# Moving the group-end output stores of a decoder-layer kernel from ScalarE to SyncE, and spreading them over the next group

## Chip, cores and metric

The kernel runs on all 8 cores of one Trainium2 chip; each core does an eighth of the tokens and shares nothing with the others. The metric is the device time of the slowest core, in microseconds (us).

An 8-core program has two states on this chip. In the fast state all cores grant TensorE a clock of about 0.98 to 0.99 of full speed on average. In the slow state the cores of one die (0 to 3 or 4 to 7) are granted less, and the whole takes some per cent longer.

## The reference

One layer over two kinds of request. Cut to what matters here:

```python
def layer(x):                                  # prompt rows, then decode rows
    n = rmsnorm(x) * norm1_g
    q, k, v, u, gates = project(n, w_in)       # u = GLU, 1024 channels
    ya = sliding_window_attention(q, k, v)     # decode rows also read cache_k, cache_v
    yc = silu(layernorm(depthwise_conv31(u)))  # decode rows also read state_conv
    h = x + (gates[0] * (ya @ w_attn_o) + gates[1] * (yc @ w_conv_o)) @ w_out
    h = h + square(relu(rmsnorm(h) @ w_up)) @ w_down
    return rmsnorm(h) * norm_f_g               # y, the output of this study
```

## The kernel before

A core works through its tokens in three groups (640, 768 and 704 columns, the last with 64 decode tokens). All activations lie transposed in SBUF: `H` is 16 chunks of 128 rows, one column a token. Weights stream through five slots in 110 slabs a group; GpSimd issues them. Each engine takes its instructions in program order, as the timelines below show. A helper adds the semaphore waits (an engine waits for a counter that another engine or a landing transfer raises) from what an operation reads and writes. For buffers in SBUF it compares byte ranges; for a tensor in DRAM it knows only the name:

```python
def keys(self, ap):
    name = ap.tensor.name
    if name not in self.base:                  # not in SBUF
        return [name]                          # one key for the whole tensor
    ...                                        # else: its 128-byte pieces
```

The 16 stores of a group write different parts of one tensor, `y`. To the helper they all write the same thing, so each store gets a wait for the landing of the store before it.

The end of a group scales `H` in place by the last norm and stores it as `y`. These tasks are put on a list, `side`, and are taken one at a time between the next group's first matmul groups (K, V, Q):

```python
def final_tasks(g):
    def fin(): ...                             # 1 / rms of H into LR
    def out(k):
        if k < 16:
            stt(H[:, k, 0:M], H[:, k, 0:M], v1(V_GF + k), LR[:, 0:M], ALU.mult, ALU.mult)   # VectorE
        if k > 0:
            P.dma("act", yo[g][:, k - 1, :], H[:, k - 1, 0:M], f"d_y{k - 1}")               # ScalarE
    return [fin] + [lambda k=k: out(k) for k in range(17)]
```

So every `step()` in K, V, Q puts one store on ScalarE's queue, between two evictions of PSUM banks:

```python
for j in range(8):                             # Q; K and V have the same form
    ...
    for c0, n in CH:
        b = fm(w, j % 2, nT, halo + c0, n)     # 16 matmuls into one of 8 PSUM banks
        act(qo[:, j, c0:c0 + n], b[:, 0:n], AF.Copy)   # ScalarE empties the bank
        step()
```

What follows K, V, Q reuses the bytes of `H`, which is why a chunk's store has a deadline:

```python
gt  = over(H, 0 ...)              # chunks 0, 1       GLU
cw  = over(H, 4096 ...)           # chunk 1           conv weights, one buffer
um  = over(H, 6144 ...)           # chunks 2 to 4     GLU outputs, three buffers
KcT = over(H, 5 * HB ...)         # chunks 5 to 7     cached keys      (last group only)
vcb = over(H, 5 * HB + 8192 ...)  # chunks 7 to 10    cached values    (last group only)
stb = over(H, 5 * HB + 16384 ...) # chunks 10 to 12   cached conv state (last group only)
tA, tB = ...                      # chunks 8 to 11, 12 to 15   gates, after GLU
```

Each of eight GLUs computes 128 channels. SyncE then makes 16 small copies (the shift), each 32 partitions, that lay the channels out for the convolution on TensorE; conv(m-1) runs behind GLU m, so a shift has one GLU's time:

```python
def sample_load():                             # last group, before GLU in this kernel
    P.dma("pool", KcT, ckT); P.dma("pool", vcb, cvT)

def glu(m):
    wl = slab() ...                            # GpSimd: load of a later slab
    ...
    for i in range(4):
        for q in range(4):
            P.dma("sp", z[32*i:32*i+32, q, 0:L-3], u[32*q:32*q+32, i:i+L-3], ...)   # shift

def conv(m):
    P.dma("pool", cw, cwd[m], "d_cw")          # GpSimd
    ...                                        # 64 or 96 matmuls

for m in range(8):
    glu(m)
    if m >= 1:
        conv(m - 1)
```

The softmax here doesn't subtract the row's maximum and nothing guards it: scores larger than these inputs give would overflow.

Of the kernel before, what the change touches and what calls it, by code (L numbers as in the profile page):

```python
# [9 lines left out]
ALU = mybir.AluOpType  # L10
# [10 lines left out]
GROUPS = [(0, 5, 128, 0), (5, 6, 0, 0), (11, 5, 0, NSMP)]  # L21
WMAX = 768
SEQW = 36
M_OUT = list(range(8)) + [10, 11, 14, 15, 8, 9, 12, 13]
ULEN = 32 + 640 + 16 * SEQW
NSLOT = 5
V_G1, V_G2, V_GF, V_BG, V_CB, V_LG, V_LB, V_SK, V_N = 0, 16, 32, 48, 80, 88, 96, 104, 120
# [134 lines left out]
def chunks_of(n):  # L162
    k = -(-n // 512)
    step = -(-n // (k * 32)) * 32
    return [(c, min(step, n - c)) for c in range(0, n, step)]


def build():
    nc = bass.Bass("TRN2", target_bir_lowering=False)
    es = ExitStack()  # L170
    with es:
# [3 lines left out]
        def dout(name, shape):  # L175
            return nc.dram_tensor(name, list(shape), F32, kind="ExternalOutput").ap()
# [15 lines left out]
        yo = [dout(f"y{i}", [128, 16 * m]).rearrange("p (k c) -> p k c", k=16) for i, (w, m) in enumerate(gw)]  # L192
# [7 lines left out]
        P = Prog(nc, es)  # L200
# [4 lines left out]
        def sb(name, shape, dt):  # L205
            t = P.sb(name, shape, dt, at[0])
            n = int(np.prod(shape[1:])) * (4 if dt == F32 else 2)
            at[0] += -(-n // G) * G
            return t
# [5 lines left out]
        H = sb("H", [128, 16, WMAX], F32)  # L215
# [8 lines left out]
        LR = sb("LR", [128, WMAX], F32)  # L224
# [59 lines left out]
        def slab(nk=16):  # L284
            k = nxt[0]
            nxt[0] += 1
            if k > 0:
                load_slab()
            t = wsl[k % NSLOT]
            return t[:, :].rearrange("p (k c) -> p k c", k=nk)  # L290
# [6 lines left out]
        def fm(w, m, act, c0, n, nk=16):  # L297

            b = bank()
            mm(b[:, 0:n], [(w[:, k, m * 128:(m + 1) * 128], act[:, k, c0:c0 + n]) for k in range(nk)])  # L300
            return b

        def act(out, in_, func, **kw):
            P.op("act", "activation", out=out, in_=in_, func=func, **kw)

        def stt(out, in0, scalar, in1, op0, op1):
            P.op("dve", "scalar_tensor_tensor", out=out, in0=in0, scalar=scalar, in1=in1, op0=op0, op1=op1)
# [4 lines left out]
        def v1(c):  # L312
            return vec[:, c:c + 1]
# [4 lines left out]
        def step(n=1):  # L318
            for _ in range(n):
                if side:  # L320
                    side.pop(0)()

        def drain():
            while side:
                side.pop(0)()
# [15 lines left out]
        def rstd(r, s, c0, n):  # L341

            b = bank()
            mm(b[:, 0:n], [(onesf[:, :], s[:, c0:c0 + n])])
            act(r[:, c0:c0 + n], b[:, 0:n], AF.Sqrt, bias=EPS)
            P.op("dve", "reciprocal", out=r[:, c0:c0 + n], in_=r[:, c0:c0 + n])

        def add_square(dst, src, first, c0, n, t=None):
            t = sq[:, c0:c0 + n] if t is None else t
            if first:  # L350
                act(dst[:, c0:c0 + n], src, AF.Square)
            else:
                act(t, src, AF.Square)
                tt(dst[:, c0:c0 + n], dst[:, c0:c0 + n], t, ALU.add)
# [11 lines left out]
        for hf in range(2):  # L366
# [3 lines left out]
            for k in range(16):  # L370
                c = slice(hf * half, hf * half + half)
                stt(nT[:, k, c], H[:, k, c], v1(V_G1 + k), R1[:, c], ALU.mult, ALU.mult)

        def norm1_tasks(g):

            W = gw[g][0]

            def p1(k):
                P.dma("sp", xr[k % 3][:, 0:W], xin[g][:, k, :], f"d_xr{k % 3}")
                add_square(R1, xr[k % 3][:, 0:W], k == 0, 0, W)  # L380

            def fin():
                for c0, n in chunks_of(W):
                    rstd(R1, R1, c0, n)

            def p2(k):
                P.dma("sp", xr[(k + 1) % 3][:, 0:W], xin[g][:, k, :], f"d_xr{(k + 1) % 3}")
                stt(nT[:, k, 0:W], xr[(k + 1) % 3][:, 0:W], v1(V_G1 + k), R1[:, 0:W], ALU.mult, ALU.mult)

            return ([lambda k=k: p1(k) for k in range(16)] + [fin] + [lambda k=k: p2(k) for k in range(16)])  # L390

        def final_tasks(g):
            M = gw[g][1]

            def fin():
                for c0, n in chunks_of(M):
                    rstd(LR, S2, c0, n)

            def out(k):
                if k < 16:  # L400
                    stt(H[:, k, 0:M], H[:, k, 0:M], v1(V_GF + k), LR[:, 0:M], ALU.mult, ALU.mult)
                if k > 0:
                    P.dma("act", yo[g][:, k - 1, :], H[:, k - 1, 0:M], f"d_y{k - 1}")

            return [fin] + [lambda k=k: out(k) for k in range(17)]

        for g, (b0, nb, halo, ns) in enumerate(GROUPS):
            first, last = g == 0, g == len(GROUPS) - 1
            W, M = gw[g]
# [104 lines left out]
            def sample_load():  # L514
                P.dma("pool", KcT[:, :, :, :], ckT[:, :].rearrange("p (a b w) -> p a b w", a=2, b=16), "d_kc")
                P.dma("pool", vcb[:, :, :], cvT[:, :].rearrange("p (b c) -> p b c", b=16), "d_vc")
# [39 lines left out]

            side += [lambda i=i, a=a: unit(i, a) for i in range(nb) for a in range(2)] + [flush]
            if last:
                sample_load()
                side += [sample_q] + [lambda a=a, hh=hh: sample_unit(a, hh) for a in range(2) for hh in range(2)]  # L560


# [2 lines left out]
            UC = chunks_of(W - us)  # L565
            L = 32 + Mp + (16 * SEQW if last else 0)
            if last:
                P.dma("pool", stb[:, :, :, :], stT[:, :].rearrange("p (k b r) -> p k b r", k=8, b=16), "d_st")

            def seqs(ap):  # L570
                return ap.rearrange("p (b r) -> p b r", r=SEQW)

            def glu(m):
                u = um[m % 3]
                wl = slab()
                if not first:
                    P.op("act", "copy", out=u[:, 0:32], in_=cuT[:, m, :])
                if last:
                    P.op("pool", "tensor_scalar", out=seqs(u[:, 32 + Mp:L])[:, :, 0:32], in0=stb[:, m, :, :],
                         scalar1=2.0, scalar2=None, op0=ALU.mult)  # L580
                for ci, (c0, n) in enumerate(UC):
                    bB = fm(wl, 0, nT, us + c0, n)
                    step(ci == 0)
                    bA = fm(wl, 1, nT, us + c0, n)
                    t = gt[ci % 2]
                    act(t[:, 0:n], bB[:, 0:n], AF.Tanh, scale=0.5)
                    pe = min(c0 + n, Mp) if last else c0 + n
                    if pe > c0:
                        stt(u[:, uoff + c0:uoff + pe], t[:, 0:pe - c0], 1.0, bA[:, 0:pe - c0], ALU.add, ALU.mult)
                    if last:  # L590
                        sv = max(c0, Mp)
                        if sv < c0 + n:
                            s0, s1 = sv - Mp, c0 + n - Mp
                            assert s0 == 0 and s1 == 64
                            stt(seqs(u[:, 32 + Mp:L])[:, :, 32:36],
                                t[:, sv - c0:n].rearrange("p (b t) -> p b t", t=4), 1.0,
                                bA[:, sv - c0:n].rearrange("p (b t) -> p b t", t=4), ALU.add, ALU.mult)
                        o0 = max(c0, Mp - 30)
                        if o0 < c0 + n:
                            stt(ucs[:, m, o0 - Mp + 30:c0 + n - Mp + 30], t[:, o0 - c0:n], 1.0, bA[:, o0 - c0:n],  # L600
                                ALU.add, ALU.mult)
                    step(ci == 1)
                if not last:
                    P.op("act", "copy", out=cuT[:, m, :], in_=u[:, Mp:Mp + 32])
                z = ush[m % 2]
                for i in range(4):
                    for q in range(4):
                        P.dma("sp", z[32 * i:32 * i + 32, q, 0:L - 3], u[32 * q:32 * q + 32, i:i + L - 3],
                              f"d_ul{m % 2}{i}{q}", merge=(i + q > 0))
# [24 lines left out]

            for m in range(8):
                glu(m)
                if m >= 1:
                    conv(m - 1)
            drain()
# [72 lines left out]

            for i, m in enumerate(M_OUT):
                if i % 2 == 0:
# [14 lines left out]
            if not last:  # L729
                side += norm1_tasks(g + 1)  # L730
            ri = 0
            for fb in range(4):
# [13 lines left out]
                for m in range(16):  # L746
# [8 lines left out]
                    if m % 2 == 1:  # L755
                        step(1)
            drain()
            side += final_tasks(g)
        drain()
        P.emit()  # L760
    return nc


def _cols(w, cols):
    k = w.shape[0] // 128
    return w[:, cols].reshape(k, 128, len(cols)).transpose(1, 0, 2).reshape(128, 4096)


def _slabs(w_in, w_ao, w_co, w_out, w_up, w_dn):
# [16 lines left out]
    for j in range(0, 16, 2):  # L786
        s.append(_cols(w_out, r(256) + M_OUT[j] * 128))
    for fb in range(4):
# [109 lines left out]
```

## Time and profile before

| | before |
|---|---|
| runs at the time of the prediction | 3565.6, 3725.5, 3942.8 us (only the first is fast) |
| profiled run, fast | 3558.2 us; cores 3539.9 to 3556.6 us |
| TensorE busy | 3376.2 us of 3556.6 |
| first border (K, V, Q of group 1), median of cores | 78.0 us |
| second border (K, V, Q of group 2) | 97.0 us |
| GLU and conv of group 1, of group 2 | 157.3 us, 162.0 us |
| the 16 last stores, after TensorE has ended | 36.2 us |

The four stage times are worked out from the timelines of the profiled run, core by core, then the median of the eight is taken. A border runs from the first matmul that sums the previous group's last norm (it sits behind K's first 16 matmuls) to ScalarE's first copy of the carried conv state; the GLU stretch goes on from there to the first matmul of the layer-norm sums.

TensorE is the bound, so what can be won is its idle time. These are the waits of TensorE in the kernel before, core 2, first in the window 1090 to 1210 us and then in 2330 to 2460 us. The columns are: engine, what it was to write, whom it waited for, us in total, number of waits, the longest.

```profile
PE ps L154 <- ACT qo L154: 7.8, 2, 6.2
PE ps L154 <- ACT vtok L154: 7.0, 1, 7.0
...
PE ps L154 <- ACT qo L154: 23.5, 4, 9.1
PE ps L154 <- ACT vst L154: 6.3, 1, 6.3
PE ps L154 <- ACT vtok L154: 1.0, 1, 1.0
```

The releaser of every wait shown is a ScalarE eviction. Why ScalarE was late is in its own timeline (start, duration, engine, operation, in brackets the idle time before and its releaser), here in the second border:

```profile
2407.89 0.34 ACTq L154 DMA_DIRECT2D y<-H  x1
2408.33 0.46 ACT L154 ACTIVATE qo<-ps 128x352 bf16<-128x352 f32 x1 [1.89 <-DMA y<-H]
2421.09 0.34 ACTq L154 DMA_DIRECT2D y<-H  x1
2421.59 0.46 ACT L154 ACTIVATE qo<-ps 128x352 bf16<-128x352 f32 x1 [12.79 <-DMA y<-H]
2434.17 0.34 ACTq L154 DMA_DIRECT2D y<-H  x1
```

A store (ACTq) stands between two evictions. Its own record takes 0.34 us, but the store issued at 2407.89 lets the next one out only at 2421.09, and the eviction behind that one stands in the queue for 12.79 us. The trace has the first landing at 2421.03. On every core of this profile, in 44 or 45 of the 45 pairs of neighbouring stores of one group, the next was issued 0.07 us after the one before had landed, and never before it. TensorE fills the eight banks and stops:

```profile
2393.34 2.55 PE L154 MATMUL ps<-nT,wsl_53 128*128 128x352 bf16 x16 [0.38 <-ACT qo L154]
2401.37 4.61 PE L154 MATMUL ps<-nT,wsl_53 128*128 128x352 bf16 x16 [5.48 <-ACT qo L154]
...
2422.20 4.44 PE L154 MATMUL ps<-nT,wsl_49 128*128 128x352 bf16 x16 [9.05 <-ACT qo L154]
```

The second line shows the other cost of a gap: 16 matmuls take 4.61 us instead of 2.55, because the clock was lowered while TensorE stood (the trace has a granted clock of one half from 2398.8 to 2405.6 us).

The timeline of GpSimd in the last group has the issue of conv 4's weights, `cw`, behind GLU 5's slab:

```profile
2523.30 0.58 POOL L154 DMA_DIRECT2D cw<-cwd  x1
```

And ScalarE's timeline ends with the last 16 stores, after TensorE's last matmul:

```profile
3517.86 36.20 ACTq L154 DMA_DIRECT2D y<-H  x16
```

### The profile page before, as it was taken

To read this page: it belongs to the slowest core of one execution; us is meant where nothing else is said; L and a number is where in the kernel's file an instruction comes from. 1 tells how busy PE (TensorE), PEld (TensorE's weight loads), DVE (VectorE), ACT (ScalarE), POOL (GpSimd) and SP (SyncE) were. 2 spreads that over 40 slices of the span, in tenths; PEclk is the share of its full clock that TensorE was granted. 3 is DMA by queue.
4 is the path that set the end of the run, shared out by engine and by line. 5 is a ranking of instruction groups with operands and counts; after the bars stand their busy time and mean duration, and the time that the engine had idled before them with its cause. 6 is when DMAs were issued, how large, how long until landed. Compare 5 with 4: busy or idle time off the path is not lost.

```text
span 3556.6 us, 61094 instructions; the slowest of 8 cores (3539.9 to 3556.6 us)
## 1 busy us (share of the span) xinstructions
PE 3376.2 (95%) x23732; PEld 2172.0 (61%) x23732; DVE 1162.6 (33%) x1846; ACT 705.5 (20%) x1381; POOL 202.3 (6%) x371
## 2 busy tenths in 40 slices
PE   2999999999999999999999999987999999999994
PEld 1656777777776455666666666654566666666663
DVE  4244133332223354224233222333542242222224
ACT  2322133111021333113211011112231131101021
POOL 0000000000000000000000000001100000000000
PEclk9999999999999999999999999998999999999997
DMA  6779877887666666556666655567776666566661
GB/s 135 118 133 174 161 149 152 161 167 136 119 122 134 125 130 143 106 115 118 137 131 132 122 99 104 101 138 156 142 153 114 126 110 113 107 112 114 108 114 71
DMA packets 98474, 453.52 MB, mean 128 GB/s; under 512 B 14960, under 2 KB 27696, under 8 KB 55472
## 3 DMA queue, kind: packets, MB, share of 16 engines
q0 software_dynamic: 51696, 355.75, 56.5%
q1 hardware_dynamic: 39584, 76.56, 8.0%
q10 hardware_dynamic: 6912, 17.30, 1.3%
q8 instruction: 195, 3.19, 0.4%
q14 instruction: 87, 0.71, 0.1%
HBM read 765.00 MB, written 23.85 MB: 222 GB/s over the span
## 4 chain that ended last, share of the span: by engine, by line
PE 89%; DMA 6%; SPq 2%; DVE 1%; issue 1%; ACT 0%; DVEq 0%; ACTq 0%
PE ps L154 89%; DMA y<-H 4%; SPq L154 2%; DMA H<-x 1%; DMA ush_83<-um_93 0%; DVE H L154 0%; DVE rden_67 L154 0%; DMA ush_82<-um_93 0%; DVE nT L154 0%; DVE LR L154 0%; DVE R_58 L154 0%; DMA ush_83<-um_94 0%; DVE um_93 L154 0%; DVE qo L154 0%; SPq L151 0%
## 5 line engine op out<-in xcount | busy, mean ns | idle before, releaser
L154 DVE TENSOR_TENSOR H<-ps,H 128x320 f32<-128x320 f32 (+2 forms) x384 | 201.5, 525 | 566.4 <-PE ps L154 566.2
L154 PE MATMUL ps<-nT,wsl_49 128*128 128x384 bf16 (+2 forms) x1344 | 217.9, 322 | 19.4 <-ACT qo L154 16.9
L154 PE MATMUL ps<-a2T,wsl_50 128*128 128x320 bf16 (+2 forms) x1344 | 203.9, 313 | 0.0
L154 PE MATMUL ps<-hb,wsl_53 128*128 128x320 bf16 (+2 forms) x1344 | 203.9, 313 | 0.0
L154 PE MATMUL ps<-a2T,wsl_51 128*128 128x320 bf16 (+2 forms) x1344 | 203.9, 313 | 0.0
L154 PE MATMUL ps<-hb,wsl_52 128*128 128x320 bf16 (+2 forms) x1344 | 203.9, 313 | 0.0
L154 PEld LDWEIGHTS ps<-nT,wsl_49 128*128 128x128 bf16 x1344 | 133.3, 100 | 101.8 <-issue 33.9
L154 ACT ACTIVATE a2T<-rt_105 128x320 bf16<-128x320 f32 (+2 forms) x96 | 47.6, 496 | 736.1 <-DVE rt_105 L154 736.1
L154 PE MATMUL ps<-nT,wsl_50 128*128 128x352 bf16 (+2 forms) x1152 | 178.9, 316 | 8.6 <-ACT qo L154 8.6
L154 PE MATMUL ps<-nT,wsl_51 128*128 128x352 bf16 (+2 forms) x1152 | 178.2, 315 | 0.5 <-issue 0.5
L154 DVE SCALAR_TENSOR_TENSOR tA<-tA,ps 128x320 f32<-128x320 f32 (+2 forms) x96 | 50.0, 520 | 387.2 <-PE ps L154 386.7
L154 PE MATMUL ps<-hb,wsl_50 128*128 128x320 bf16 (+2 forms) x1152 | 175.3, 313 | 0.0
L154 PE MATMUL ps<-a2T,wsl_49 128*128 128x320 bf16 (+2 forms) x1152 | 174.8, 313 | 0.0
L154 PE MATMUL ps<-a2T,wsl_52 128*128 128x320 bf16 (+2 forms) x1152 | 174.8, 313 | 0.0
L154 PE MATMUL ps<-hb,wsl_51 128*128 128x320 bf16 (+2 forms) x1152 | 174.8, 313 | 0.0
L154 PE MATMUL ps<-a2T,wsl_53 128*128 128x320 bf16 (+2 forms) x1152 | 174.8, 313 | 0.0
L154 PE MATMUL ps<-hb,wsl_49 128*128 128x320 bf16 (+2 forms) x1152 | 174.8, 313 | 0.0
L154 PEld LDWEIGHTS ps<-hb,wsl_52 128*128 128x128 bf16 x1344 | 131.5, 98 | 69.4 <-issue 0.4
L154 PEld LDWEIGHTS ps<-a2T,wsl_50 128*128 128x128 bf16 x1344 | 131.5, 98 | 69.0
L154 PEld LDWEIGHTS ps<-hb,wsl_53 128*128 128x128 bf16 x1344 | 131.5, 98 | 69.0
L154 PEld LDWEIGHTS ps<-a2T,wsl_51 128*128 128x128 bf16 x1344 | 131.5, 98 | 69.0
L154 PE MATMUL ps<-nT,wsl_52 128*128 128x352 bf16 (+2 forms) x960 | 152.5, 320 | 14.3 <-ACT vtok L154 8.0
(222 smaller groups left out, 4284.0 us busy)
## 6 DMA issues: line engine op xcount, KB each, us to landing
wsl_49<-wst POOLq DMA_DIRECT2D x66, 1024.0 KB, 9.5
wsl_50<-wst POOLq DMA_DIRECT2D x66, 1024.0 KB, 9.5
wsl_51<-wst POOLq DMA_DIRECT2D x66, 1024.0 KB, 9.4
wsl_52<-wst POOLq DMA_DIRECT2D x66, 1024.0 KB, 9.8
wsl_53<-wst POOLq DMA_DIRECT2D x66, 1024.0 KB, 9.5
H<-x SPq DMA_DIRECT2D x8, 768.0 KB, 21.6
cw<-cwd POOLq DMA_DIRECT2D x24, 256.0 KB, 8.6
H<-x SPq DMA_DIRECT2D x16, 384.0 KB, 7.2
```

The lines of the kernel that those rows point to most:

```text
L154: i = getattr(eng, ins[0])(**ins[1])
```

## The change

The intent is to take the stores off ScalarE, which TensorE depends on, and to put them on SyncE, which has next to nothing to do in K, V, Q. Eight stores go there, in the order in which the next group needs the bytes: chunks 0 to 4 for GLU, 10 to 12 for the conv state. The other eight go out one behind each shift. Because `KcT` and `vcb` lie over chunks 5 to 10, of which 5 to 9 are now stored during GLU, their loads move behind GLU 5.

```diff
+Y_OUT = [0, 1, 2, 3, 4, 10, 11, 12, 5, 6, 7, 8, 9, 13, 14, 15]
...
+        stores = []
+        def store():
+            if stores:
+                stores.pop(0)()
...
-            def out(k):
-                if k < 16:
-                    stt(H[:, k, 0:M], ...)
-                if k > 0:
-                    P.dma("act", yo[g][:, k - 1, :], H[:, k - 1, 0:M], f"d_y{k - 1}")
-            return [fin] + [lambda k=k: out(k) for k in range(17)]
+            def out(i, k):
+                stt(H[:, k, 0:M], ...)
+                stores.append(lambda: P.dma("sp", yo[g][:, k, :], H[:, k, 0:M], f"d_y{k}"))
+                if i < 8:
+                    store()
+            return [fin] + [lambda i=i, k=k: out(i, k) for i, k in enumerate(Y_OUT)]
...
             if last:
-                sample_load()
                 side += [sample_q] + ...
...
             for m in range(8):
                 glu(m)
+                store()
+                if last and m == 5:
+                    sample_load()
                 if m >= 1:
                     conv(m - 1)
...
         drain()
+        while stores:
+            store()
```

More of the change, by code (lines that the diff above doesn't have):

```diff
@@ L397, in fin @@
                     rstd(LR, S2, c0, n)
-            def out(k):
-                if k < 16:
-                    stt(H[:, k, 0:M], H[:, k, 0:M], v1(V_GF + k), LR[:, 0:M], ALU.mult, ALU.mult)
-                if k > 0:
-                    P.dma("act", yo[g][:, k - 1, :], H[:, k - 1, 0:M], f"d_y{k - 1}")
-            return [fin] + [lambda k=k: out(k) for k in range(17)]
+            def out(i, k):
+                stt(H[:, k, 0:M], H[:, k, 0:M], v1(V_GF + k), LR[:, 0:M], ALU.mult, ALU.mult)
+                stores.append(lambda: P.dma("sp", yo[g][:, k, :], H[:, k, 0:M], f"d_y{k}"))
+                if i < 8:
+                    store()
+            return [fin] + [lambda i=i, k=k: out(i, k) for i, k in enumerate(Y_OUT)]
         for g, (b0, nb, halo, ns) in enumerate(GROUPS):
```

## The prediction

> Times are for the fast state: of the runs before (3565.6, 3725.5, 3942.8 us) only the first is fast, as is the profiled one (3558). I predict against about 3560, not the median.
>
> **What bounds it.** The summary shows TensorE 95% busy (3376 of 3557 us). It idles about 65 us at the start, 42 after its last matmul, 46 at the two group borders, 17 waiting for conv shifts. The chain of waits puts 4.2% (149 us) on y stores, but TensorE works through most of that; only its idle counts.
>
> In the TensorE waits at the borders (K, V, Q of the next group) the releaser is a ScalarE eviction (vtok, vst, qo): 15 us at the first, 31 us at the second. The ScalarE timeline shows a y store between evictions, and the next instruction often comes only when a store has landed (2.2 us undisturbed, 8 to 13 beside weight loads).
>
> After each gap over 5 us matmuls run slowly: 16 of 352 columns take 4.6 instead of 2.55 us. The Trainium skill (TensorE: Matmul & The Clock Gate, HAM section) says that an idle window of about 3.4 us halves the clock; this trace agrees (granted clock 0.90 and 0.85 in the two stretches). That costs 4.7 and 7.9 us. To be won: 19 + 39 = 58 us on the slowest core, some 50 on others.
>
> **What the change does.** The stores leave ScalarE; else TensorE, ScalarE and VectorE keep their order. SyncE is nearly idle in K, V, Q, so eight stores there are free. Bytes stay the same. It adds:
> 1. SyncE in GLU: a shift (16 copies) occupies it 10.6 to 12.7 us; shifts start every 16 to 19 us, but the last every 13.2 us, when attention has run out. A store of 2.3 to 8 us fits the long gaps, not the last two or three, where TensorE already waits (1 to 3 us each). Estimate: +6 us in group 1, +5 in group 2, at conv 5 to 7.
> 2. Last group: the loads of KcT and vcb move behind GLU 5 on GpSimd's queue, ahead of conv 4's weights (cw). vcb must wait for the store of chunk 9, behind shift 4 (which ended at 2530 us). cw, issued at 2523 us before, is issued near 2535 and lands behind 1 MB loads: from before's landings (16.8, 23.2, 29.2 us, some 7 us apart) I estimate 2546, while conv 4 is due at 2533. A stall of 12 us (10 more than before) plus 3 of low clock: +13 us.
> 3. End: 16 stores on ScalarE took 36 us; on SyncE I expect the same.
>
> **Sum.** 58 - 11 - 13 = 34 us on the slowest core, a little less on others: 3528 us (0.9% faster), 8 in 10 between 3500 and 3556. Faster by over 2%: 3%; within 2%: 95%; slower by over 2%: 2%.
>
> **To check.** TensorE waits on vtok, vst, qo near zero at both borders, clock there about 1.0; K, V, Q with GLU's first matmuls in about 65 and 61 us (before 84 and 97). Waits on ush grow by 2 to 8 us each at the late convs. In the last group one TensorE wait of 8 to 20 us at conv 4, released by cw. Final stores 36 us.
>
> **What would make it wrong.** Stores in GLU much slower than 5 us would push every shift back (up to 30 us lost, no gain). cw may overtake the cache loads, or vcb be issued early (45 to 50 us gained). Final stores could be slower on SyncE. If the slow state falls on most runs, times are hundreds of us higher for other reasons.

## The result

| | before | after |
|---|---|---|
| runs, all | 3559.5, 3565.6, 3725.5, 3942.8 us | 3526.4, 3529.8, 3530.4, 3531.4 us |
| median of all | 3645.6 us | 3530.1 us |
| ratio of fast runs | 1 | 0.9907 (95% interval 0.9883 to 0.9931) |
| cores in the profiled run | 3539.9 to 3556.6 us | 3509.9 to 3528.9 us |
| first border | 78.0 us | 61.6 us |
| GLU stretch of group 1 | 157.3 us | 158.0 us |
| second border | 97.0 us | 58.0 us |
| GLU stretch of group 2 | 162.0 us | 187.0 us |
| last 16 stores | 36.2 us | 35.4 us |

The ratio is the mean time of one kernel's fast runs over that of the other's of the same rounds, so it is not quite the ratio of the medians quoted. The medians of all runs differ by 3%, but two of the four runs before were slow and none of the four after; the change is worth 0.9%.

The stages account for it: 16.4 + 39.0 = 55.4 us won at the borders, 0.7 lost in the first GLU stretch and 25.0 in the second, 29.7 us in all; the medians of the cores' spans in the two profiled runs, about 3548 and 3521 us, differ by 27.

In the profile after, TensorE of core 6 (the slowest) waits for nothing between 1095 and 1175 us, nor between 2300 and 2400 us: the lists of waits are empty. The first border is an unbroken row of matmuls at full clock; three lines of it, from the timeline of TensorE, without any idle time in brackets:

```profile
1131.04 10.56 PE L155 MATMUL ps<-nT,wsl_51 128*128 128x384 bf16 x64
1141.44 10.56 PE L155 MATMUL ps<-nT,wsl_52 128*128 128x384 bf16 x64
1151.84 10.56 PE L155 MATMUL ps<-nT,wsl_53 128*128 128x384 bf16 x64
```

A new wait stands first among the rest of TensorE's waits in the whole run (the start of the kernel left out):

```profile
PE ps L155 <- DMA cw<-cwd: 22.1, 1, 22.1
PE ps L155 <- DMA ush_83<-um_93: 10.4, 3, 6.8
...
PE ps L155 <- DVE ucs L155: 3.2, 1, 3.2
```

All eight cores have it, with 18.8 to 22.8 us. TensorE's timeline shows that it is conv 4, and what follows at low clock (5.04 us; conv 3, with data at hand, took 2.72):

```profile
2470.16 2.72 PE L155 MATMUL ps<-ush_83,cw 128*32 128x320 bf16 x96
...
2505.79 5.04 PE L155 MATMUL ps<-ush_82,cw 128*32 128x320 bf16 x96 [22.11 <-DMA cw<-cwd]
```

GpSimd's timeline shows what `cw` waited for:

```profile
2471.00 0.58 POOL L155 DMA_DIRECT2D KcT<-ckT  x1
2493.09 0.53 POOL L155 DMA_DIRECT2D vcb<-cvT  x1 [21.52 <-issue]
2493.65 0.53 POOL L155 DMA_DIRECT2D cw<-cwd  x1
```

GpSimd stood 21.5 us before it issued `vcb`. It calls the wait "issue", that is, it names no releaser; the chain of waits in the window 2465 to 2512 us names it: the store of chunk 9, which SyncE had issued behind shift 4 and whose bytes `vcb` reuses, and then `cw` behind the cache loads. (Columns: start, us, what.)

```profile
2481.21 8.87 DMA y<-H
2490.11 2.96 issue
...
2493.65 11.47 DMA cw<-cwd
```

SyncE's timeline in GLU of group 1 shows why the stores there cost so little, and its last line the final 16 stores:

```profile
1118.26 44.62 SPq L155 DMA_DIRECT2D y<-H  x8
...
1293.48 11.97 SPq L155 DMA_DIRECT2D ush_82<-um_92  x16
1305.54 0.54 SPq L155 DMA_DIRECT2D y<-H  x1
1306.71 11.51 SPq L155 DMA_DIRECT2D ush_83<-um_93  x16
...
3488.61 35.36 SPq L155 DMA_DIRECT2D y<-H  x16
```

Eight stores in a row hold SyncE for 44.62 us, 5.6 us each. But a single store between two shifts holds it for 0.54 us, and the next shift starts 0.6 us after it. The difference is the helper's wait again. Seven of the eight stores in a row wait for the one before, at line 152 of the kernel, the helper's `wait_ge`; of the final sixteen, fifteen do (SyncE's own waits, core 6, first in the window 1100 to 1190 us, then in 3480 to 3530):

```profile
SPq L152 <- DMA y<-H: 40.7, 7, 9.6
...
SPq L152 <- DMA y<-H: 27.5, 15, 2.0
```

A store in GLU finds that the one before has long landed. The queue itself is not what holds: the 16 copies of a shift, which the helper does not chain, went out 0.75 us apart (from 1293.48 us), while each landed 3.3 to 9.5 us after its issue.

### The profile page after: what moved, and what is told of

It is laid out like the page before. It is cut to its first block, busy times and chain, and to the rows that moved or that the text cites. A ratio compares the mean times of both kernels' runs of the same rounds, so it can differ in the third digit from the quotient of the medians.

```text
span 3528.9 us, 61086 instructions; the slowest of 8 cores (3509.9 to 3528.9 us)
## 1 busy us (share of the span) xinstructions
PE 3366.7 (95%) x23732; PEld 2169.5 (61%) x23732; DVE 1162.5 (33%) x1846; ACT 706.5 (20%) x1381; POOL 202.5 (6%) x371
## 4 chain that ended last, share of the span: by engine, by line
PE 90%; DMA 4%; SPq 2%; DVE 2%; issue 1%; ACT 0%; DVEq 0%; POOL 0%; ACTq 0%; POOLq 0%
PE ps L155 90%; DMA y<-H 2%; SPq L155 2%; DMA H<-x 1%; DVE rden_67 L155 0%; DVE H L155 0%; DMA ush_83<-um_93 0%; DMA cw<-cwd 0%; DMA stb<-stT 0%; DMA ush_83<-um_94 0%; DVE nT L155 0%; DVE LR L155 0%; DMA ush_82<-um_92 0%; DVE R_58 L155 0%; DVE rden_68 L155 0%
## 5 line engine op out<-in xcount | busy, mean ns | idle before, releaser
L155 PEld LDWEIGHTS ps<-nT,wsl_49 128*128 128x128 bf16 x1344 | 132.0, 99 | 81.4 <-issue 13.3
L155 PE MATMUL ps<-nT,wsl_51 128*128 128x352 bf16 (+2 forms) x1152 | 178.2, 315 | 0.0
L155 PE MATMUL ps<-nT,wsl_50 128*128 128x352 bf16 (+2 forms) x1152 | 176.7, 313 | 0.0
L155 PEld LDWEIGHTS ps<-nT,wsl_51 128*128 128x128 bf16 x1152 | 112.5, 98 | 63.3 <-issue 3.7
```

Source lines behind the costliest of these rows:

```text
L155: i = getattr(eng, ins[0])(**ins[1])
```

## The experiments

Theory A says that the borders were long because stores on ScalarE held up evictions; its rival B says that too much was stored in that stretch, whichever engine issued it. Theory C says that the loss in the last group is `cw` standing behind `vcb`, which waits for a store, plus crowding of the DMA engines by the cache loads; its rival D says crowding alone. Three chips served three batches of runs. On the first, even runs counted as fast had dips of clock on a die, the kernel before lying between 3559 and 3599 us; there the stage times of the profiled run say more than the total. The stage times, in us, medians of the cores of one profiled run each:

| kernel | border 1 | GLU 1 | border 2 | GLU 2 |
|---|---|---|---|---|
| before | 78.0 | 157.3 | 97.0 | 162.0 |
| changed | 61.6 | 158.0 | 58.0 | 187.0 |
| changed, run again | 62.1 | 157.6 | 58.0 | 187.2 |
| stores on ScalarE, spread | 69.7 | 158.2 | 72.1 | 177.2 |
| before, stores on SyncE | 61.6 | 175.5 | 58.0 | 198.5 |
| cw first | 61.6 | 157.4 | 58.0 | 172.4 |
| chunk 9 early | 61.6 | 158.1 | 58.0 | 181.2 |
| loads apart, early | 62.2 | 158.6 | 58.4 | 176.3 |
| the same, two queues at the end | 62.0 | 157.7 | 58.3 | 176.8 |
| loads apart, late | 61.6 | 157.8 | 58.0 | 168.5 |
| no cache loads | 61.6 | 158.9 | 58.0 | 175.5 |

### Stores at the new places, but on ScalarE

```diff
-                stores.append(lambda: P.dma("sp", yo[g][:, k, :], ...))
+                stores.append(lambda: P.dma("act", yo[g][:, k, :], ...))
```

> The changed kernel with its stores, at the same places, issued from ScalarE again. Theory A (what counts at the borders is that a store on ScalarE holds up the evictions behind it): eight of sixteen stores still sit between evictions, so some of the border waits come back, TensorE waits on vtok, vst, qo of about 7 us in each border plus low clock, about 19 us for both against 58 before; the wait on cw stays near 20 us; 3540 to 3555 us. Rival B (the gain is that half the stores left the border, whatever engine issues them): no border waits to speak of, 3525 to 3535 us, like the changed kernel.

Measured: ratio to the kernel before 0.9893 (0.9837 to 0.9949); its quiet runs took 3540.3, 3542.0 and 3542.5 us. The waits in the second border, core 7:

```profile
PE ps L155 <- ACT vst L155: 6.1, 1, 6.1
PE ps L155 <- ACT vtok L155: 4.6, 1, 4.6
```

Part of the border loss came back: 8.1 us and 14.1 us over the changed kernel, 22.2 us together against the 19 expected. With half the stores gone from the border but the engine unchanged, about 40% of the loss remains. This speaks for A and against B. In GLU the same stores on ScalarE cost nothing that the table shows (158.2 us in group 1): there the store before has landed.

One expectation failed: the wait on `cw` was not near 20 us but 13.4 to 17.3 us on the eight cores, and the second GLU stretch took 177.2 us, 9.8 less than in the changed kernel. On ScalarE the store of chunk 9 did not stand behind the copies of shift 4: it went out 1.5 us before `KcT`, and in the changed kernel some 10 us after it. This agrees with theory C.

### The kernel before, only the engine changed

```diff
-                    P.dma("act", yo[g][:, k - 1, :], H[:, k - 1, 0:M], f"d_y{k - 1}")
+                    P.dma("sp", yo[g][:, k - 1, :], H[:, k - 1, 0:M], f"d_y{k - 1}")
```

> The kernel before with one word changed: all sixteen stores stay in K, V, Q but are issued from SyncE; cache loads stay where they were. Theory A: the border waits on vtok, vst, qo vanish (58 us won on the slowest core), but the stores occupy SyncE for about 16 x 5.5 = 88 us, longer than the 64 us of K, V, Q, so the first conv shifts start late: about 10 us lost in group 1; in the last group KcT, vcb and stb load late too, about 25 us lost at the first conv. 3520 to 3555 us, with waits on ush at conv 0. Rival B: the same bytes in the same stretch, so no gain, 3555 us or more, with TensorE still waiting in K, V, Q.

Measured: ratio 0.9964 (0.9911 to 1.0017), its quickest run 3556.7 us. The borders are those of the changed kernel to the tenth (61.6 and 58.0 us), with all sixteen stores still issued in a row. That settles A against B: it is enough that the stores, with their waits for each other, leave ScalarE. Not tested is the other remedy, to let the helper tell the chunks of `y` apart and to leave the stores on ScalarE. But SyncE now issues stores until long after the border, and the shifts queue behind them (first the timeline of SyncE, core 7, group 1, then TensorE's waits in that GLU stretch):

```profile
1117.27 99.45 SPq L154 DMA_DIRECT2D y<-H  x16
1216.91 33.03 SPq L154 DMA_DIRECT2D ush<-um  x35
```

```profile
PE ps L154 <- DMA ush<-um: 26.2, 3, 23.7
```

Sixteen stores took 99.45 us and the first shift began at 1216.91. GLU lost 18.2 us in group 1 and 36.5 us in group 2 (in the latter also because the cache loads came late), which is 54.7 of the 55.4 won. So the second half of the change, the spreading, is what keeps the gain. The expectation had 10 and 25 us; the stores in a row, each issued when the one before had landed, were slower (6.2 us each) than the 5.5 assumed.

### Conv weights ahead of the cache loads

```diff
                 store()
-                if last and m == 5:
-                    sample_load()
                 if m >= 1:
                     conv(m - 1)
+                if last and m == 5:
+                    sample_load()
```

> The changed kernel with the loads of KcT and vcb one place later on GpSimd's queue, behind conv 4's cw. Theory C (cw is late because it stands behind vcb, which waits for the store of chunk 9): the wait of 22 us on cw is gone, but vcb itself still waits for that store until about 2490 us and lands about 10 us later, while the first sample unit needs it near 2491: a new wait of about 10 us on vcb. Net 8 to 14 us faster than the changed kernel: 3514 to 3522 us. Rival D (the DMA engines are simply overfull in this stretch): cw stays late by over 10 us, no gain.

Measured: ratio 0.9865 (0.9809 to 0.9920) in a noisy batch, with 3519.5 us in the only run in which both dies were undisturbed. The wait on `cw` is gone (core 4, window 2400 to 2600 us):

```profile
PE ps L155 <- DMA ush<-um: 7.7, 2, 5.1
PE ps L155 <- DMA vcb<-cvT: 1.2, 1, 1.2
```

The GLU stretch fell from 187.0 to 172.4 us, with 174.1 on the die that was undisturbed in the profiled run. So the place of `cw` in GpSimd's queue was about half of the loss of 25.0 us (see the repeat below), against D. A miss of size: the wait on `vcb` was at most 4.1 us on any core, not 10; about 5 us moved to the shift of conv 4, which now shares the DMA engines with the cache loads.

Run again in the third batch:

> The run with cw ahead of the cache loads once more, so that the next two can be compared with it on one chip. It should repeat: last group's GLU stretch (from the first copy of carried conv state to the layer-norm sums) 172 us against 187 in the changed kernel and 162 before; on an undisturbed die about 10 us shorter than the changed kernel's 3521.

Its three fast runs took 3518.5, 3519.2 and 3521.0 us, ratio 0.9876 (0.9856 to 0.9895). The profiled execution was slow, so it is not in the table. But its die 0 (cores 0 to 3) was undisturbed, with a clock of 0.988: the GLU stretch of group 2 took 175.6 us there, not the 172 expected. With both profiles the order of the loads is worth 11 to 15 of the 25 us.

### Chunk 9 stored early

```diff
-Y_OUT = [0, 1, 2, 3, 4, 10, 11, 12, 5, 6, 7, 8, 9, 13, 14, 15]
+Y_OUT = [0, 1, 2, 3, 4, 10, 11, 12, 9, 5, 6, 7, 8, 13, 14, 15]
-                if i < 8:
+                if i < 9:
```

> The changed kernel with chunk 9 stored ninth, still in K, V, Q, so that vcb needs no store behind shift 4; the loads stay ahead of cw. Theory C: vcb is issued right after KcT (about 2471 us), cw about 2472 us; cw still queues behind the slab and both cache loads and lands near 2494: the wait on cw falls from 22 to about 10 us. 8 to 14 us faster than the changed kernel: 3514 to 3522 us. If the whole stall was the wait for the store, it falls below 3 us (3505 us); if it was all queueing, it stays near 20 us.

Measured: ratio 0.9836 (0.9783 to 0.9890), verdict unclear. Four runs without a disturbed die took 3526.7 to 3528.3 us, only 2 to 3 us below the changed kernel's 3530 on another chip, where 8 to 14 were expected; the GLU stretch is 5.8 us shorter. GpSimd no longer waits for the store: `vcb` follows `KcT` after 2.2 us. Yet conv 4 still waits 14.6 us (13.4 to 15.7 on the eight cores), now with the shift named (core 4; TensorE's waits, then GpSimd's timeline):

```profile
PE ps L155 <- DMA ush<-um: 16.8, 3, 14.6
```

```profile
2472.28 0.58 POOL L155 DMA_DIRECT2D KcT<-ckT  x1
2474.48 0.53 POOL L155 DMA_DIRECT2D vcb<-cvT  x1 [1.63 <-issue]
2475.04 0.53 POOL L155 DMA_DIRECT2D cw<-cwd  x1
```

A shift copy issued at 2481.20 us took 19.1 us to land, and `cw` needed 19.3 us, beside a slab and both cache loads, where the medians of the same operations are 8.7 and 9.1 us over the whole stretch (2400 to 2560 us). So crowding is real, too: with the store out of the way, it alone makes a wait of this length. The store wait and the queueing overlap, and the 22 us cannot be split into two parts that add up. The Trainium skill (DMA: Bandwidth & Descriptors, section Queues, rings and completion order) says that a DMA engine goes round the queues that have work, packet by packet, so small copies on another queue share it with large loads; these landings agree, but no run here looks at packets.

### Both remedies: the loads earlier, together or apart

These ran in a second batch, beside the changed kernel once more:

> The changed kernel itself, unedited, once more, to stand beside the next three on the same chip. Both theories: one wait on cw of 19 to 23 us on every core, no wait on vtok, vst or qo; 3526 to 3535 us in fast runs if the chip is as steady as the first one.

Its five fast runs took 3536.0 to 3548.9 us (ratio 0.9913, 0.9873 to 0.9952), and the wait on `cw` was 23.0 us on core 2. The first ratio repeats.

First both loads behind conv 3's `cw`, with chunk 9 early:

```diff
                 if m >= 1:
                     conv(m - 1)
+                if last and m == 4:
+                    sample_load()
```

> Chunk 9 stored ninth, and both cache loads together one GLU earlier, behind conv 3's cw. Theory C (store wait plus crowding): the wait for the store is gone, but 2 MB of cache in the same stretch as a slab and a shift still crowd the copies of that shift, as in the run with chunk 9 early, where one shift copy took 19 us to land: a wait on ush of 3 to 10 us at conv 3 or 4, no wait on cw over 3 us. 15 to 22 us faster than the changed kernel of these rounds. If crowding doesn't matter, no wait over 3 us there.

Five fast runs took 3526.0 to 3532.2 us, in the mean about 12 us below the changed kernel, not 15 to 22. Its profile is of no use: that execution took 17,195 us for reasons that its trace does not tell, so the waits stay unknown.

Then the loads apart, `KcT` behind conv 2's `cw` and `vcb` behind conv 3's:

```diff
+                if last and m == 3:
+                    load_kc()
+                if last and m == 4:
+                    load_vc()
```

> As the run before this one, but the loads apart: KcT behind conv 2's cw, vcb behind conv 3's. Theory C: one extra MB a GLU fits beside slab and shift; waits on ush and cw in the last group's conv 3 and 4 stay under 3 us each; 22 to 27 us faster than the changed kernel of these rounds, about 3505 us. If it is the number of bytes in all that crowds the shifts, it is no better than the loads together.

Six fast runs took 3527.9 to 3535.9 us, about 11 us below the changed kernel: a miss of half, and no better than the loads together. The GLU stretch is 176.3 us. GpSimd's timeline of core 0 shows that the loads were put too early for the stores that they depend on:

```profile
2454.51 0.53 POOL L155 DMA_DIRECT2D KcT<-ckT  x1 [12.91 <-DMA y<-H]
...
2477.77 0.53 POOL L155 DMA_DIRECT2D vcb<-cvT  x1 [18.57 <-DMA y<-H]
```

GpSimd stood 12.9 us for the store of chunk 7 and 18.6 us for that of chunk 8, and the slabs and `cw` behind them were late again (a wait on `cw` of 3.8 us on this core).

### Two queues for the last stores

```diff
-    stores.append(lambda: P.dma("sp", yo[g][:, k, :], ...))
+    stores.append(lambda: P.dma("act" if g == len(GROUPS) - 1 and i % 2 else "sp", yo[g][:, k, :], ...))
```

> The run before this one, and the last group's sixteen final stores alternate between SyncE and ScalarE. In both profiles these stores take 35 to 36 us from one queue, at a DMA share under 0.4, 2.2 us apart. If one queue's issue is the limit, two queues side by side end them in about 20 us: 14 to 17 us faster than the split run. If the DMA engines or the memory behind them are the limit, no change.

Five fast runs took 3524.9 to 3529.3 us; the mean is about 3 us below the run without this edit, and not 14 to 17. The stores on the two queues take as long together as those on one queue did. The first fence has the timelines of SyncE and of ScalarE on core 1, the second the table of busy times in that window: the window, its length, five engines with their instructions, the clock, the DMA share and GB/s.

```profile
3484.52 33.92 SPq L155 DMA_DIRECT2D y<-H  x8
...
3487.43 33.34 ACTq L155 DMA_DIRECT2D y<-H  x8
```

```profile
3484.00:3520.00 36.00, 0.00 (x0) 0.00 (x0) 13.09 (x16) 0.00 (x0) 0.00 (x0) 0.50 0.38 150
```

From the first issue to the end of the last, 3484.5 to 3520.8, it is 36.3 us; the run without this edit took 35.9 from one queue on the same core. The DMA engines were busy 0.38 of the time at 150 GB/s; with one queue it was 0.39 and 152. The expectation named one queue's issue, the DMA engines or the memory as the limit; the traces show a fourth. The stores did not run side by side: the helper chains them across the queues, and on this core ScalarE's first store went out at 3487.43, after SyncE's first had landed at 3487.36, and so on in turn. One store of 360 KB in flight at a time, some 2.3 us from one to the next, gives about 157 GB/s (an estimate from these two figures), close to the 150 measured. The Trainium skill (DMA: Bandwidth & Descriptors, section Issuing engines are not separate DMA queues) says that starting transfers from several engines saves only the time to issue them; this run does not test it. How fast the 16 stores would end without the chain is open.

### The loads apart, one GLU later

```diff
+                if last and m == 4:
+                    load_kc()
+                if last and m == 5:
+                    load_vc()
```

with chunk 9 early, as above.

> Chunk 9 ninth, KcT behind conv 3's cw and vcb behind conv 4's, each one GLU later than in the split run. There GpSimd stood 13 us waiting for the store of chunk 7 and 17 us for that of chunk 8 and held up slab and cw behind it; here both stores landed a GLU earlier. Theory C: GpSimd doesn't wait for a store, no wait on cw at all, waits on ush at conv 3 and 4 below 4 us each; the GLU stretch takes 166 to 172 us; 3500 to 3510 us on an undisturbed die. If the crowding alone made the loss, it stays at 172 to 177 us like the split run.

Two fast runs, 3511.3 and 3517.5 us, ratio 0.9861 (0.9838 to 0.9885), beside 3560.3 to 3567.4 us of the kernel before on that chip. GpSimd issues both loads without waiting for a store, right behind `cw` (core 4):

```profile
2448.93 0.58 POOL L155 DMA_DIRECT2D cw<-cwd  x1 [2.79 <-PE ps L155]
2449.55 0.53 POOL L155 DMA_DIRECT2D KcT<-ckT  x1
...
2473.25 0.68 POOL L155 DMA_DIRECT2D cw<-cwd  x1 [9.21 <-PE ps L155]
2473.92 0.54 POOL L155 DMA_DIRECT2D vcb<-cvT  x1
```

On all eight cores TensorE never waits for `cw`, and its waits on the shift at conv 3 and 4 are 0 to 2.3 us. The GLU stretch is 168.5 us, as expected and the shortest of all kernels with the changed stores; the total is 1 to 8 us above the 3500 to 3510 expected. By its stages this is the best version tried; it is 1.4% under the kernel before. That it beats the changed kernel rests on the stage; the totals, by the ratios (0.9861 and 0.9907) 0.5% apart, come from different chips, with two fast runs here.

### Without the cache loads

The two loads of the run before are replaced by VectorE memsets.

> Wrong on purpose: the run before, with both cache loads replaced by VectorE memsets, so that 2 MB of transfers are gone and nothing else. Theory C: without their bytes the shifts and cw land as in the kernel before, no wait on cw, waits on ush as before; GLU stretch about 162 to 165 us, so the y stores themselves cost at most 3 us. If the y stores on SyncE cost more, as the prediction had it (5 us in this group), the stretch is 167 us or more.

Fast runs 3516.5 to 3519.5 us; the outputs are wrong. The stretch took 175.5 us, not 162 to 165. The experiment did not do its job: a memset took 3.5 us on VectorE, and TensorE waited 4.2 us for it, in the middle of the stretch. What can be read is that no wait on `cw` appears and that conv 3 and conv 4 wait 0 and 1.3 us for their shifts on the two cores looked at. How much of the last 6.5 us between the late split (168.5) and the kernel before (162.0) is crowding stays open. Part of it is something else: in the late split TensorE waits 1.8 to 5.7 us (median 3.6) for VectorE's writes of `ucs` and `qo`, where the kernel before has 0.6 us on every core; the next section says why.

## Why the prediction was right or wrong

- **The total.** 3528 us was predicted and 3530.1 us measured, a gain of 0.9% in the fast state in both.
- **The borders.** 58 us were to be won on the slowest core, some 50 on others: measured 55.4 (median). TensorE's waits there vanished, and the clock is 1.00 in both. The mechanism, that evictions wait behind stores, is shown by the run that changed the engine alone. Why the stores wait, for each other by the helper's semaphores, the prediction did not ask. The Trainium skill (TensorE: Matmul & The Clock Gate, HAM section) says that the clock is halved after an idle window of about 3.4 us; the after profile agrees too: after 22 us of waiting, conv 4 took 5.04 us instead of 2.72.
- **The stores in GLU ("+6 us in group 1, +5 in group 2").** This term failed. Group 1 lost 0.7 us. The step behind it was that a store occupies SyncE until it lands ("a store of 2.3 to 8 us"); it was read from stores in a row, where it looks so (44.62 us for eight). In fact a store waits for the landing of the store before it, because the helper takes `y` as one object. In GLU that one had landed long before: seven of the eight stores held SyncE for 0.52 to 0.54 us and one for 1.26 (core 6, group 1), and landings of 2.8 to 4.3 us did not stop the next shift.
- **The wait on cw ("+13 us").** Right in place, releaser and kind, too small in size: conv 4 waited 18.8 to 22.8 us, not 12, and the second GLU stretch lost 25.0 us, not 18. The mis-sized step is the store of chunk 9. The prediction let `vcb` go some 5 us after the end of shift 4; on core 6 it went 12 us after (store issued at 2481.21, `vcb` at 2493.09). The store took 8.9 us to land (6.8 to 9.2 on the eight cores), and `vcb` went out 3.0 us after that, on every core. That the landing was slow because a slab and `KcT` shared the DMA engines is likely and not tested. The part behind it was well sized: `cw` landed 11.5 us after its issue, 11 were expected.
- **What it left out.** Crowding as a cost of its own: with the store out of the way, conv 4 still waited 14.6 us. And a smaller one: the load of the conv state waits for the store of chunk 12, the last of the eight in a row, and TensorE waited 3.2 us for VectorE's write behind it on core 6 (up to 5.1 on three others, next to nothing on four). The traces name the links (on core 6 GpSimd stood 16.8 us for a store before it issued the load of `stb`, and then VectorE for GpSimd's write from it); no run tests them.
- **The end.** 36 us were expected to stay: 35.4 us. The chain of the stores is the same on either engine.

By stages, 6 us were predicted for the first GLU stretch and 0.7 measured; 18 (5 for the stores, 13 for `cw`) for the second and 25.0 measured. The errors had opposite signs, so the sum came out right: that it met the total within about 2 us is luck. The total alone would not have shown it.

## What to carry to other kernels

Keep a transfer that has to wait for something off the queue of an engine that others wait for: a store's record may be 0.3 us long while its wait holds everything behind it for 2 to 13 us. Ask first whether the wait is needed. Here each store waited for the one before, which wrote other bytes, because a helper saw one name; telling the chunks apart may have won the borders, and part of the 36 us at the end, without moving a store, but no run tried it. And before a queue is blamed for a gap, look for a semaphore wait in the program: `prof` lists SyncE's own waits with their line. When a store is spread out over a later stage, look at each load that reuses its bytes: in an in-order queue, that load's wait becomes the wait of whatever stands behind it, here small weights that were due soon. Put the urgent small load ahead, and place the large one where its store has landed a stage before.

## What the Trainium skill lacked or had wrong

- DMA: Bandwidth & Descriptors, section Issuing engine by pattern, names Sync for plain loads and stores, and treats sync and scalar as alike. It lacks the price of choosing ScalarE when ScalarE also evicts PSUM and the stores have to wait: 55.4 us in two borders here, won back to the tenth by the engine alone (78.0 to 61.6 and 97.0 to 58.0 us).
- The same page, section Queues, rings and completion order, says how queues share a DMA engine, but not what this does to small copies: beside 3 MB of loads a shift copy took 19.1 us to land, against a median of 8.7 us over the whole stretch.
